# A fused transformer stack on one core: experts' first products between the quarters of a gather, and an embedding gate in unsplit full precision

## The chip, the core and the metric

The kernel runs on one core of a Trainium2 chip. Five engines work side by side, each through its own list of instructions in order: TensorE (PE; its weight loads are listed as PEld), VectorE (DVE), ScalarE (ACT), GpSimd (POOL) and SyncE (SP), which here only issues the transfers from memory (DMA). They wait for each other by semaphores. The metric is device time of one execution, in microseconds (us). Three runs of the kernel before took 1017.16, 1017.79 and 1019.13 us; the median is 1017.79.

## The reference

256 tokens (two blocks of 128) of width 1024, float32, go through five stages, each named by its result: a gated delta rule mixer with layernorm (x1), a mixture of experts with layernorm (x2), an embedding gate (x3), an "even" layer of mLSTM and pooling (x4) and an "odd" layer of sparse attention (the output). The change touches the second and third:

```
# mixture of experts: best of 4 groups, then the 2 best of its 8 experts
comb = g_onehot[:, :, None] * within[:, None, :]
for grp in range(MOE_GROUPS):
    h = silu(einsum("td,edf->tef", xt, w_gate[grp])) * einsum("td,edf->tef", xt, w_up[grp])
    out = out + einsum("tef,efd->td", h * comb[:, grp, :, None], w_down[grp])
x = _layernorm(DEEPNORM_ALPHA * x + h, ln_g[i, 1], ln_b[i, 1])                   # x2
x = x + jax.nn.sigmoid(x @ pe_w_gate[i]) * (p[i] @ pe_w_proj[i])                 # x3
```

## The kernel before

All stages are one program. Its order is not written out by hand: when the program is built, small generators (one for each piece of work) run under a planner that keeps a model clock for each engine and, where several pieces could go next, takes the one of the best number in the table `PRIO` (lower first; L40). What it decides becomes the fixed list of each engine.

**Weights** come in units of 128x1024 float32 (512 KB). `_load` (L518) walks through the list of all units in order: each waits for a free place (tiles named `raw`, `hl`, `first`, `moe_raw` (shown as la, xh_raw, xl_raw or moe_raw), `moe_hl`; the trace's names are those of the places), and SP issues its transfer. Because SP keeps the order of the list, a unit that waits for a place holds all behind it. Most weights are then split by `_split` (L542) into a high part in the rounded type fp32r (a cast, on ACT or DVE) and the low rest (a subtract, on DVE or POOL), and a product x@W is made of three fp32r products: high by high, low by high, high by low. A unit marked `full` isn't split and enters PE as float32, in full precision: the experts' units are of that kind.

**Mixture of experts.** The experts are worked on in eight sets of four, two for each group. `gather` (four quarters c per group) collects the tokens of the group's experts by products with a selection matrix `sel`, and copies each quarter into the tiles X. `back` transposes `sel` for the way back. `up(i)` runs over four steps j: each needs four units `m_gu` and quarter j of the gathered tokens, does eight products and gives the four places free. `down(i)` does the same with eight units `m_dn`, `scatter` brings the results back to the tokens and, after the last set, sums up for the layernorm that gives x2. `S.quiet` (L2285) tells `_split` to stay away from certain engines until an event.

**Embedding gate.** `Embed.main` takes eight units `p_gate`, `turn` transposes x2 in halves of 512 columns for each block of tokens and splits it into `xh` (ACT) and `xl` (DVE), and `block_slabs` does, per block of tokens (tb), 4 slabs x 8 steps of three fp32r products 128x256, 192 in all. `Embed.out` adds the gate to x2. The event `parted` lets no unit of the even layer be split before all `p_gate` units have their split's places. `e_v`, `e_za`, `e_qk` are the first units of the even layer.

In the trace, L207 are PE's products, L227 its transposes, L130 the operations of ACT, DVE and POOL, L178 ACT's table loads, and L232 the transfers.

Of the kernel before, what the change touches and what calls it, by code (L numbers as in the profile page):

```python
# [10 lines left out]
F32 = mybir.dt.float32  # L11
F32R = mybir.dt.float32r
I32 = mybir.dt.int32
AF = mybir.ActivationFunctionType
# [9 lines left out]
def size(ap):  # L24
# [14 lines left out]
}  # L39
PRIO = {  # L40
    "decay": [2, 3], "pick": 4, "base": 1, "lev": 1, "solve": 7, "qk": [2, 3], "v": 5, "z": 6,
    "m_turn": 2, "ranks": 1, "gather": 4, "back": 4, "slot_w": 6, "rest": 6, "act_out": 1, "scatter": 3,
    "m_const": 2, "parts": 1, "router": 3, "norm2": 1, "e_turn": 1, "embed": 7, "e_gates": 1, "gated": 2,
    "e_const": 2, "tokens": 3, "e_head": 3, "e_conv": 3, "window": 0, "e_out": 1, "keys": 1, "normed": 2,
    "copy": 2, "o_head": 2, "o_const": 2, "select": 2, "attend": 3, "o_gate": 1, "queries": 1, "o_out": 1,
# [6 lines left out]
QUIET = 0  # L52
QUIET_ON = [("dve", "pool"), ("dve",)]
SECOND = 15
SCRATCH = 1024
COST = {"parts": 2.5, "decay": 0.4, "conv": 2.8, "conv_qk": 3.0, "conv_v": 0.0, "gate": 0.65}

# [346 lines left out]
class Unit:  # L404
# [4 lines left out]
    def __init__(self, name, src, more="", n=1024, whole=False, late=False, full=False,  # L409
                 places=None):  # L410
        self.name, self.src, self.more, self.n, self.whole, self.late = name, src, more, n, whole, late
        self.full, self.low, self.places = full, False, places or ("raw", more + "raw", *(["first"] if more == "moe_" else []))
        self.sent, self.loaded, self.parted = Event(), Event(), Event()
        self.ready = self.loaded if whole or full else Event()
        self.raw = self.h = self.l = None

# [4 lines left out]
class Env:  # L421


    def __init__(self, tc, aps, ctx):
# [9 lines left out]
        S.slot_class("hl", self.wp, 6)  # L434
        S.slot_class("bank", self.psp, 4)
        S.slot_class("dbank", self.psp, 4)

    def gate_slots(self):

        s = self.S.slots  # L440
        s["gate_hl"] = s["moe_raw"] + s["moe_hl"]
        self.S.pools["gate_hl"] = self.S.pools["moe_raw"]
        held = [x for _, x in self.S.held.values() if x.cls in ("moe_raw", "moe_hl")]
        for x in s["gate_hl"] + held:
            x.cls = "gate_hl"
        self.S.drop("moe_raw", "moe_hl")

    def consts(self):
        nc, c, aps = self.nc, self.const, self.a
# [91 lines left out]

    def _split(self, u):  # L542
        S = self.S
        if u.more == "even_":

            yield Wait(*[v.parted for v in self.units[0:u.index] if v.more == "gate_"])
        hl = yield Alloc(("hl", u.more + "hl"), [1024], F32R, 2)
        S.set(u.parted)
        yield Wait(u.loaded)
        if u.full:  # L550
            S.free(*hl)
            return
        u.h, u.l = hl
        if u.more in ("moe_", "gate_"):

            late = Event()
            late.time = u.loaded.time + S.tune["slack"]
            yield Wait(late)
        near = u.index - self.at <= 1
        e = yield from self.outside(u, act=0.96, dve=0.61 + S.tune["high"][near])  # L560
        if u.full:
            S.free(*hl)
            return
        h, l, raw = u.h[:, 0:u.n], u.l[:, 0:u.n], u.raw[:, 0:u.n]
        if e == "act":
            S.s.activation(h, raw, AF.Copy)
        else:
            S.v.tensor_copy(h, raw)
        near = u.index - self.at <= 1
        e = yield from self.outside(u, dve=1.14 + S.tune["low"][near], pool=2.3)  # L570
        if u.full:
            S.free(*hl)
            return
        u.low = True
        S.of(e).tensor_tensor(l, raw, f32(h), op=OP.subtract)
        S.free(u.raw)
        S.set(u.ready)
# [1485 lines left out]
class Moe:  # L2063
# [215 lines left out]
    def scatter(self, i, y):  # L2279
        K, S = self.K, self.S  # L2280
        g, q = divmod(i, 2)
        last = i == 7
        if last:
            yield Wait(*self.done[0:7])
            S.quiet = QUIET_ON[1], ("p_gate",), self.bn_ev[1]  # L2285
            for n in range(2):
                S.spawn(self.start(0, n), "scatter")
        ys = yield Alloc("ys", [2, 512], F32R, 2)
        yield "act"
        for n in range(2):  # L2290
            S.s.activation(ys[0][:, n], y[n], AF.Copy)
        for n in range(2):
            yield "dve"
            S.v.tensor_tensor(ys[1][:, n], y[n], f32(ys[0][:, n]), op=OP.subtract)
            S.free(y[n])
        yield Wait(self.r_ev, self.selT_ev[g])
        selT = self.selT[g]
        for tb in range(2):
            for n in range(2):
                if last:  # L2300
                    yield Wait(self.sum_ev[tb][n])
                    p = self.sum[tb][n]
                else:
                    p = yield Alloc("bank", [512])
                yield "pe"
                for a in range(2):
                    S.mm(p, selT[:, q, tb, :], ys[a][:, n], a == 0 and not last, a == 1)
                if last:
                    S.set(self.sc_ev[tb][n])
                    if tb == 0:  # L2310
                        S.spawn(self.start(1, n), "scatter")
                    continue
                yield "dve"
                r = self.r[tb][:, 512 * n:512 * n + 512]
                S.v.tensor_tensor(r, r, p, op=OP.add)
                S.free(p)
        S.free(*ys)
        if q == 1:
            S.free(self.selT.pop(g))
# [130 lines left out]
def moe_units(a, K):  # L2450
    def unit(name, src):
        return Unit(name, src, "moe_", full=True, places=RAWS)

    def gu(i):
        return [unit("m_gu", lambda h=h, j=j: a["m_gu"][4 * i + h, :, 2 * j:2 * j + 2])
                for j in range(4) for h in range(4)]

    def dn(i):
        return [unit("m_dn", lambda h=h, k=k: a["m_dn"][4 * i + h, :, k]) for k in range(2) for h in range(4)]

    out = [Unit("m_r", lambda: a["m_r"], "moe_", 288, True)]
    for i in range(9):
        if i == 6:
            out += [Unit("pT", lambda: a["pT"], "moe_", 512, True)]
            out += [Unit("p_proj", lambda k=k: a["p_proj"][0, :, k], "moe_", whole=True) for k in range(2)]
        if i == 7:
            out += [Unit("lnr", lambda j=j: K.ln_row(1, j), "moe_", 1024, True) for j in range(2)]
        out += (gu(i) if i < 8 else []) + (dn(i - 1) if i > 0 else [])
    return out + [Unit("p_gate", lambda i=i, h=h: a["p_gate"][i, :, 4 * h:4 * h + 4], "gate_", places=("raw", "first")) for i in range(4) for h in range(2)]


class Embed:
# [6 lines left out]
        self.x_free = Event()  # L2479

    def turn(self, tb, c, x, ev):
        yield Wait(self.M.x2_ev[tb])
        yield from self.K.turn(self.M.x2[tb], tb, *x, 4 * c, ev)

    def main(self):
        K, S = self.K, self.S
        self.x2, self.pp = self.M.x2, self.M.E.pp
        x = K.parts()
        ev = [Event() for _ in range(4)]
        for tb in range(2):  # L2490
            for c in range(2):
                S.spawn(self.turn(tb, c, x, ev[2 * tb + c]), "e_turn")
        done = []
        yield from K.block_slabs(["p_gate"] * 4, x, ev,
                                 lambda i, tb, bank: done.append(S.spawn(self.out(i, tb, bank), "embed")))
        S.set(self.x_free)
        yield Wait(*done)
        S.free(self.x2, self.pp)

# [506 lines left out]
def build(tc, aps, upto="out", start="x1"):  # L3006
    nc = tc.nc
    run = ORDER[ORDER.index(start):ORDER.index(upto) + 1]
    with ExitStack() as ctx:
# [33 lines left out]
        if "x2" in run:  # L3043
            S.tune = TUNE["x2"]
            if "x1" not in run:
                K.moe_slots()
                E = Entry(K)
                E.lg = E.tile("lg", [2, 36])
                nc.sync.dma_start(E.lg, aps["lg"])
                for e in E.x1_ev + E.lg_ev:  # L3050
                    e.time = 0.0
                E.start(x)
            with ExitStack() as st:
                M = Moe(K, st, E)
                done = S.spawn(M.main(), 5)
                S.run(done)
                K.gate_slots()
                x, x_ev, free = M.x2, [[e, e] for e in M.x2_ev], ev[0]
                if "x3" in run:
                    E = Embed(K, M)  # L3060
                    x, x_ev, free = E.x3, E.x3_ev, E.x_free
                    if "x4" in run:
                        inp = K.rms_input(x, x_ev, "e_norm", free)
                    S.run(S.spawn(E.main(), 1))
                else:
                    S.run(M.x2_ev[0])
                    S.run(M.x2_ev[1])
                S.drop(*M.classes)
            S.drop("gate_hl", "first")
            K.moe_ctx.close()  # L3070
            K.first_ctx.close()
        S.tune = TUNE["x4"]
# [40 lines left out]
```

## Time and profile before

| | |
|---|---|
| median of three runs | 1017.79 us |
| profiled execution, its own time | 1019.82 us |
| its span (first to last instruction) | 1018.0 us |
| mean clock granted to PE | 0.973 |
| busy: PE, DVE, ACT, POOL | 956.3, 612.6, 485.1, 136.4 us |
| moved by DMA | 205.39 MB, mean 202 GB/s |

The profile is of one execution. Its busy times are sums over stages with different limits, so they don't tell what a stage waits for; the windows (busy time of each engine in a stretch, PE's granted clock, where 1.00 is 2.4 GHz and 0.50 is 1.2 GHz, DMA's share and rate) and the timelines do. In a timeline a row is one instruction or a run of like ones, with its start, its duration, and in square brackets the idle time ahead of it on its engine and what ended that. A full-precision product leaves two records in the trace. The stages lie about as follows: x1 to 360 us, the experts to 592, the embedding gate to 624, the even layer to some 900, the odd layer to the end.

### The profile page before, as it was taken

Reading aid. Unit: us, or ns where it says so; the run is one execution under the profiler, and the core shown is the slowest. Engines: PE = TensorE matmul, PEld = TensorE weight load, DVE = VectorE, ACT = ScalarE, POOL = GpSimd, SP = SyncE. Lnnn points to the kernel's source line nnn. Section 1 sums busy time; section 2 is a strip of 40 time slices with the busy share of each in tenths; the row PEclk is TensorE's granted clock in tenths of the full one; section 3 lists DMA queues with packets and bytes.
Section 4 is the critical chain, followed back from the end, with each engine's and each line's share of the span. In section 5 each row is a group of like instructions: output and inputs, shape, how many; then the busy total and the mean of one; then the engine's idle time right before and its main releaser. Section 6 shows DMA issues by size and latency. Waiting matters only on the chain. (4 is left out here: it accounts for less than half of the span.)

```text
span 1018.0 us, 17221 instructions
## 1 busy us (share of the span) xinstructions
PE 956.3 (94%) x6841; PEld 734.4 (72%) x6841; DVE 612.6 (60%) x1132; ACT 485.1 (48%) x904; POOL 136.4 (13%) x140
## 2 busy tenths in 40 slices
PE   8999879999799999999887889999999999998998
PEld 7778768888588754424221268999999988986886
DVE  7978964689956531221111287697677756587673
ACT  3888584893245222111100156566665444546561
POOL 2233232312000000000000081000000000005230
PEclk9999979999899989999998979999999999999999
DMA  6423411133738599999999853544444555633221
GB/s 224 146 83 105 163 33 56 63 104 125 277 106 327 212 369 397 409 409 409 408 410 407 334 194 117 179 164 156 160 146 166 166 185 164 255 111 104 84 95 51
DMA packets 56680, 205.39 MB, mean 202 GB/s; under 512 B 6416, under 2 KB 6800, under 8 KB 56208
## 3 DMA queue, kind: packets, MB, share of 16 engines
q1 hardware_dynamic: 56304, 204.02, 54.8%
q8 instruction: 56, 0.92, 0.4%
q14 instruction: 32, 0.26, 0.1%
q10 hardware_dynamic: 288, 0.19, 0.1%
HBM read 203.14 MB, written 1.05 MB: 201 GB/s over the span
## 5 line engine op out<-in xcount | busy, mean ns | idle before, releaser
L207 PE MATMUL dbank<-xh,hl 128*128 128x256 f32 x1072 | 217.0, 294 | 0.0
L207 PEld LDWEIGHTS dbank<-xh,hl 128*128 128x128 f32 x1072 | 172.7, 192 | 7.5 <-issue 5.8
L207 PE MATMUL dbank<-xl,hl 128*128 128x256 f32 x536 | 151.9, 283 | 0.0
L130 DVE TENSOR_TENSOR hl<-raw,hl 128x1024 fp32r<-128x1024 f32 x100 | 122.7, 1233 | 37.2 <-ACT hl L130 34.9
L130 ACT ACTIVATE hl<-raw 128x1024 fp32r<-128x1024 f32 x90 | 94.8, 1057 | 71.0 <-PE dbank L207 44.3
L207 PE MATMUL dbank<-hl,xh 128*128 128x256 f32 (+1 forms) x512 | 121.2, 321 | 1.0 <-ACT xh L130 1.0
L207 PEld LDWEIGHTS dbank<-xl,hl 128*128 128x128 f32 x536 | 103.0, 192 | 4.2 <-issue 4.1
L207 PEld LDWEIGHTS dbank<-hl,xh 128*128 128x128 f32 x512 | 89.2, 200 | 8.2 <-issue 1.9
L207 PE MATMUL dbank<-hl,xl 128*128 128x256 f32 (+1 forms) x256 | 80.9, 316 | 0.9 <-DVE xl L130 0.8
L178 ACT ACT_TABLE_LOAD x51 | 65.4, 1283 | 0.9
L207 PE MATMUL dbank<-first,raw 128*128 128x256 f32 (+1 forms) x260 | 61.7, 402 | 0.2 <-DMA first<-in_m_gu 0.2
L130 POOL TENSOR_TENSOR hl<-raw,hl 128x1024 fp32r<-128x1024 f32 x16 | 38.6, 2414 | 117.7 <-ACT hl L130 111.7
L207 PEld LDWEIGHTS dbank<-hl,xl 128*128 128x128 f32 x256 | 51.3, 200 | 3.7 <-DVE xl L130 1.4
L207 PEld LDWEIGHTS dbank<-first,raw 128*128 128x128 f32 (+1 forms) x260 | 47.0, 185 | 8.9 <-DMA first<-in_m_gu 1.8
L130 DVE TENSOR_TENSOR t<-t,t 128x31 f32<-128x31 f32 (+15 forms) x124 | 47.7, 385 | 4.3
L130 DVE SCALAR_TENSOR_TENSOR h<-h,cg,dbank 128x256 f32<-128x256 f32 x8 | 3.8, 480 | 77.1 <-ACT h L130 77.1
L130 DVE TENSOR_TENSOR moe_raw_m<-moe_raw_m,bank 128x512 f32<-128x512 f32 x28 | 18.9, 685 | 47.8 <-PE bank L207 47.8
L130 ACT ACTIVATE h<-dbank 128x256 f32<-128x256 f32 x16 | 5.9, 382 | 79.8 <-PE dbank L207 79.7
L130 DVE TENSOR_TENSOR ys<-dbank,ys 128x512 fp32r<-128x512 f32 x16 | 10.9, 689 | 46.4 <-ACT ys L130 46.2
L130 POOL TENSOR_TENSOR hl<-la,hl 128x1024 fp32r<-128x1024 f32 x3 | 7.1, 2371 | 228.0 <-DMA la<-in_p_gate 228.0
L130 ACT ACTIVATE ys<-dbank 128x512 fp32r<-128x512 f32 x16 | 9.4, 597 | 50.3 <-PE dbank L207 39.8
L207 PE MATMUL bank<-sel,x 128*128 128x256 f32 x128 | 32.1, 410 | 0.6 <-DVE sel L130 0.6
(512 smaller groups left out, 2136.0 us busy)
## 6 DMA issues: line engine op xcount, KB each, us to landing
la<-in_m_gu SPq DMA_DIRECT2D x40, 512.0 KB, 10.2
first<-in_m_gu SPq DMA_DIRECT2D x23, 512.0 KB, 10.2
hl<-in_m_gu SPq DMA_DIRECT2D x20, 512.0 KB, 10.2
moe_raw_m<-in_m_gu SPq DMA_DIRECT2D x20, 512.0 KB, 10.2
raw<-in_g_qk SPq DMA_DIRECT2D x16, 512.0 KB, 4.9
raw<-in_g_z SPq DMA_DIRECT2D x16, 512.0 KB, 3.5
raw<-in_g_v SPq DMA_DIRECT2D x16, 512.0 KB, 3.5
moe_raw_m<-in_m_dn SPq DMA_DIRECT2D x16, 512.0 KB, 10.1
```

The lines of the kernel that those rows point to most:

```text
L130: r = f(*a, **k)
L178: self.nc.scalar.preload_act_table_set(t)
L207: self.nc.tensor.matmul(out, lhsT, rhs, start=first, stop=last, skip_group_check=True)
```

## The change

Two things. In `PRIO`, `gather` goes from 4 to 6 and `back` from 4 to 7, so that the planner prefers an expert's products (priority 5, that of `Moe.main`) to the next quarter of the gather and to the transposes. And the units `p_gate` become `full`: they aren't split, `turn` transposes x2 and makes one float32 copy of each half (ACT or DVE) in place of `xh` and `xl`, and `main` does 64 products 128x256 in float32 itself. With this `parted` and `gate_slots` go (splits of the even layer no longer wait for those of the gate), and `S.quiet` after the last set of experts now keeps DVE and POOL from splitting `e_v` and `e_za` until the second block's statistics are done.

```diff
-    "m_turn": 2, "ranks": 1, "gather": 4, "back": 4, "slot_w": 6, ...
+    "m_turn": 2, "ranks": 1, "gather": 6, "back": 7, "slot_w": 6, ...
...
+PLACES = ("first", "moe_raw", "moe_hl")
...
     def _split(self, u):
         S = self.S
-        if u.more == "even_":
-
-            yield Wait(*[v.parted for v in self.units[0:u.index] if v.more == "gate_"])
         hl = yield Alloc(("hl", u.more + "hl"), [1024], F32R, 2)
-        S.set(u.parted)
...
-            S.quiet = QUIET_ON[1], ("p_gate",), self.bn_ev[1]
+            S.quiet = QUIET_ON[0], ("e_v", "e_za"), self.bn_ev[1]
...
-    return out + [Unit("p_gate", ..., "gate_", places=("raw", "first")) ...]
+    return out + [Unit("p_gate", ..., "gate_", full=True, places=PLACES) ...]
...
     def turn(self, tb, c, x, ev):
+        S, x2 = self.S, self.M.x2[tb]
         yield Wait(self.M.x2_ev[tb])
-        yield from self.K.turn(self.M.x2[tb], tb, *x, 4 * c, ev)
+        p = yield Alloc("bank", [4, 128])
+        yield "pe"
+        for i in range(4):
+            S.tr(p[:, i], x2[:, 512 * c + 128 * i:512 * c + 128 * i + 128], self.K.ident)
+        o = x[:, :, 128 * tb:128 * tb + 128]
+        e = yield Any(act=0.6, dve=0.69)
+        if e == "act":
+            S.s.activation(o, p, AF.Copy)
+        else:
+            S.v.tensor_copy(o, p)
+        S.free(p)
+        S.set(ev)
...
-        yield from K.block_slabs(["p_gate"] * 4, x, ev,
-                                 lambda i, tb, bank: done.append(S.spawn(self.out(i, tb, bank), "embed")))
-        S.set(self.x_free)
+        banks = yield Alloc("dbank", [2, 256], n=4)
+        us = [[K.unit("p_gate") for _ in range(2)] for _ in range(4)]
+        for tb in range(2):
+            for i, bank in enumerate(banks):
+                for half, u in enumerate(us[i]):
+                    yield Wait(u.ready, ev[2 * tb + half])
+                    w = u.raw.rearrange("p (k n) -> p k n", k=4)
+                    yield "pe"
+                    for k in range(4):
+                        S.mm(bank[:, tb], x[half][:, k, 128 * tb:128 * tb + 128], w[:, k], k == half == tb == 0,
+                             half == 1 and k == 3)
+                    if tb:
+                        S.free(u.raw)
+                done.append(S.spawn(self.out(i, tb, bank), "embed"))
```

The planner turns this into other lists of instructions. On PE, at the first group's gather, the list was as follows before (bank is a quarter of the gather, dbank the sum of the first set of experts, first and la are places of weight units, moe_raw_m the gathered tokens):

```order
L207 MATMUL bank_3701<-sel_3632,x_3280 128x256 x4
L207 MATMUL bank_3702<-sel_3632,x_3280 128x256 x4
L207 MATMUL bank_3703<-sel_3632,x_3280 128x256 x4
L207 MATMUL bank_3720<-sel_3632,x_3280 128x256 x4
L227 MATMUL bank_3726<-identr,sel_3632 128x128 x4
L207 MATMUL dbank_3635<-first_2728,moe_raw_m_3630 32x512 x2
L207 MATMUL dbank_3635<-la_3195,moe_raw_m_3630 32x512 x2
```

and is now:

```order
L208 MATMUL bank_3701<-sel_3632,x_3280 128x256 x4
L208 MATMUL bank_3702<-sel_3632,x_3280 128x256 x2
L208 MATMUL dbank_3635<-first_2728,moe_raw_m_3630 32x512 x2
L208 MATMUL dbank_3635<-la_3195,moe_raw_m_3630 32x512 x2
L208 MATMUL dbank_3635<-first_2728,moe_raw_m_3630 32x512 x2
L208 MATMUL dbank_3635<-la_3195,moe_raw_m_3630 32x512 x2
L208 MATMUL bank_3702<-sel_3632,x_3280 128x256 x2
L208 MATMUL bank_3703<-sel_3632,x_3280 128x256 x2
L208 MATMUL dbank_3635<-la_3195,moe_raw_m_3630 32x512
```

A quarter and a half are gathered, then the eight products of step j=0 follow, and the rest of the gather is mixed with the next steps; the transposes of `sel` come later.

On ACT, behind the sums of the last set of experts, the list was (st_6289 and st_6290 are the statistics of the first and the second block of tokens, la, first and moe_hl are units `p_gate` and their parts, xh<-bank the cast of the transposed x2):

```order
L130 ACTIVATE st_6289<-st_6289,eps_97 128x1
L130 ACTIVATE st_6289<-st_6289 128x1
L130 ACTIVATE moe_hl_6374<-first_2728 128x1024
L130 ACTIVATE first_2728<-dbank_6337,st_6289 128x320
L130 ACTIVATE moe_raw_m_6376<-first_2728 128x1024
L130 ACTIVATE moe_raw_m_6378<-la_3195 128x1024
L130 ACTIVATE moe_raw_m_6380<-la_3195 128x1024
L130 ACTIVATE xh<-bank_6393 128x4x128
L130 ACTIVATE xh<-bank_6394 128x4x128
```

and is now, with raw_6245 and raw_6255 the two units `e_v`, raw_6262 the first `e_za`, and moe_hl_6367<-bank_6377 the copy of the first half of the transposed x2:

```order
L131 ACTIVATE st_6289<-st_6289 128x1
L131 ACTIVATE first_2728<-dbank_6337,st_6289 128x320
L131 ACTIVATE hl_6259<-raw_6245 128x1024
L131 ACTIVATE hl_6293<-raw_6255 128x1024
L131 ACTIVATE st_6290<-st_6290,eps_97 128x1
L131 ACTIVATE st_6290<-st_6290 128x1
L131 ACTIVATE moe_hl_6367<-bank_6377 128x4x128
L131 ACTIVATE hl_6309<-raw_6262 128x1024
```

The casts of `p_gate` are gone, and the casts of both `e_v` stand ahead of the second block's statistics and of the copy.

On PE, at the start of the gate, two sets of four transposes and fp32r products in threes stood (hl_6259 and hl_6260 are a unit's high and low part):

```order
L227 MATMUL bank_6393<-identr,first_2728 128x128 x4
L227 MATMUL bank_6394<-identr,first_2728 128x128 x4
L207 MATMUL dbank_6389<-hl_6259,xh 128x256
L207 MATMUL dbank_6389<-hl_6259,xl 128x256
L207 MATMUL dbank_6389<-hl_6260,xh 128x256
L207 MATMUL dbank_6389<-hl_6259,xh 128x256
```

and now full-precision products in fours (la and first as moving operand are unsplit units, moe_hl_6367 and first_2728 as the other the halves of x2):

```order
L228 MATMUL bank_6377<-identr,first_2728 128x128 x4
L228 MATMUL bank_6378<-identr,first_2728 128x128 x4
L208 MATMUL dbank_6373<-la_3243,moe_hl_6367 128x256 x4
L208 MATMUL dbank_6373<-la_3243,first_2728 128x256 x4
L208 MATMUL dbank_6374<-la_3299,moe_hl_6367 128x256 x4
L208 MATMUL dbank_6374<-first_2728 128x256 x4
L208 MATMUL dbank_6375<-first_2728,moe_hl_6367 128x256 x4
L208 MATMUL dbank_6375<-la_3195,first_2728 128x256 x4
L208 MATMUL dbank_6376<-la_3195,moe_hl_6367 128x256 x4
L208 MATMUL dbank_6376<-la_3243,first_2728 128x256 x4
L228 MATMUL bank_6409<-identr,la_3320 128x128 x4
L228 MATMUL bank_6410<-identr,la_3320 128x128 x4
```

Each slab of the first block takes its two units one after the other, and the second block's transposes stand behind the first block's last product.

## Rows read from the trace of the kernel before

**Rows 1.** Page: the 40 slices (25.45 us each), data rate.

```profile
GB/s 224 146 83 105 163 33 56 63 104 125 277 106 327 212 369 397 409 409 409 408 410 407 334 194 117 179 164 156 160 146 166 166 185 164 255 111 104 84 95 51
```

**Rows 2.** Windows by stage; columns: busy us of each engine, clock, DMA share, GB/s.

```profile
386.00:576.00 190.00, 171.54 (x874) 56.30 (x872) 34.34 (x58) 25.55 (x57) 0.00 (x0) 0.98 1.03 409
595.20:601.70 6.50, 6.31 (x28) 6.02 (x29) 3.98 (x4) 4.10 (x7) 5.68 (x5) 0.50 0.43 173
601.70:623.80 22.10, 21.33 (x176) 20.91 (x176) 19.54 (x23) 9.45 (x19) 9.15 (x4) 1.00 0.23 74
631.90:900.00 268.10, 267.31 (x1960) 251.72 (x1959) 188.29 (x296) 147.41 (x237) 0.74 (x5) 1.00 0.52 174
900.00:1018.00 118.00, 108.33 (x671) 89.75 (x670) 77.65 (x163) 58.80 (x130) 33.50 (x39) 0.99 0.25 85
```

**Rows 3.** Chain of waits near the gate's end; columns: start us, us, what.

```profile
610.91 12.95 PE dbank L207 x106
```

**Rows 4.** SP timeline, the gather; columns: start us, us, engine, line, operation, tiles, count.

```profile
366.44 0.33 SPq L232 DMA_DIRECT2D xh_raw<-in_m_gu  x1
376.14 0.80 SPq L232 DMA_DIRECT2D first<-in_m_gu  x2
```

**Rows 5.** PE timeline, the gather of group 0 (records, two to a product).

```profile
363.64 10.20 PE L207 MATMUL bank<-sel,x 128*128 128x256 f32 x32 [0.55 <-DVE sel L130]
...
374.20 0.62 PE L207 MATMUL dbank<-first,moe_raw_m 128*32 128x512 f32 x2
...
382.07 7.17 PE L207 MATMUL bank<-sel,x 128*128 128x256 f32 x32
```

**Rows 6.** Windows at the gather of group 0.

```profile
370.00:374.00 4.00, 4.00 (x21) 3.51 (x20) 0.00 (x0) 1.32 (x3) 0.00 (x0) 1.00 1.02 411
374.00:386.00 12.00, 12.00 (x93) 5.77 (x92) 0.00 (x0) 3.62 (x6) 0.00 (x0) 1.00 0.83 292
```

**Rows 7.** ACT timeline, the copy of the gather's first quarter.

```profile
367.45 0.60 ACT L130 ACTIVATE moe_raw_m<-bank 128x512 f32<-128x512 f32 x1 [3.44 <-PE bank L207]
```

**Rows 8.** ACT timeline, the start of the gate.

```profile
588.46 1.06 ACT L130 ACTIVATE hl<-la 128x1024 fp32r<-128x1024 f32 x1 [0.61 <-DMA la<-in_p_gate]
589.42 0.28 ACT L130 ACTIVATE st<-st,eps 128x1 f32<-128x1 f32 x1
589.73 0.20 ACT L130 ACTIVATE st<-st 128x1 f32<-128x1 f32 x1
...
594.62 1.06 ACT L130 ACTIVATE xh<-bank 128x512 fp32r<-128x512 f32 x2
```

**Rows 9.** PE timeline, the gate: transposes, first product, second half's transposes, a wait.

```profile
592.06 1.33 PE L227 MATMUL bank<-identr,first 128*128 128x128 f32 x5 [2.49 <-DVE first L130]
...
595.25 0.58 PE L207 MATMUL dbank<-hl,xh 128*128 128x256 f32 x1 [0.62 <-ACT xh L130]
...
607.16 0.60 PE L227 MATMUL bank<-identr,la 128*128 128x128 f32 x4
...
608.38 0.51 PE L207 MATMUL dbank<-moe_raw_m,xh 128*128 128x256 f32 x2 [0.38 <-POOL moe_raw_m L130]
```

**Rows 10.** SP timeline, transfers for the stage behind the gate.

```profile
585.53 1.62 SPq L232 DMA_DIRECT2D raw<-in_e_v  x2
588.51 28.01 SPq L232 DMA_DIRECT2D raw<-in_e_za  x2
```

**Rows 11.** DMA issues from 578 to 600 us, with median time to landing.

```profile
raw<-in_e_v SPq DMA_DIRECT2D x2, 512.0 KB, 10.6
```

**Rows 12.** Windows where the queue of transfers ends.

```profile
596.00:597.00 1.00, 1.00 (x5) 1.00 (x6) 1.00 (x2) 1.00 (x2) 1.00 (x1) 0.50 1.00 401
597.00:598.00 1.00, 1.00 (x6) 1.00 (x6) 1.00 (x1) 0.05 (x1) 1.00 (x1) 0.50 0.86 344
```

**Rows 13.** DVE timeline, the statistics of the first half of x2.

```profile
587.83 0.21 DVE L130 BATCH_NORM_AGGREGATE st<-st 128x2 f32<-128x12 f32 x1
```

**Rows 14.** PE timeline, full-precision products 128x256 early in the kernel.

```profile
8.03 3.62 PE L207 MATMUL dbank<-first,raw 128*128 128x256 f32 x16
```

More of the change, by code (lines that the diff above doesn't have):

```diff
@@ L41 @@
     "decay": [2, 3], "pick": 4, "base": 1, "lev": 1, "solve": 7, "qk": [2, 3], "v": 5, "z": 6,
-    "m_turn": 2, "ranks": 1, "gather": 4, "back": 4, "slot_w": 6, "rest": 6, "act_out": 1, "scatter": 3,
+    "m_turn": 2, "ranks": 1, "gather": 6, "back": 7, "slot_w": 6, "rest": 6, "act_out": 1, "scatter": 3,
     "m_const": 2, "parts": 1, "router": 3, "norm2": 1, "e_turn": 1, "embed": 7, "e_gates": 1, "gated": 2,
@@ L412, in __init__ @@
         self.full, self.low, self.places = full, False, places or ("raw", more + "raw", *(["first"] if more == "moe_" else []))
-        self.sent, self.loaded, self.parted = Event(), Event(), Event()
+        self.sent, self.loaded = Event(), Event()
         self.ready = self.loaded if whole or full else Event()
@@ L436, in __init__ @@
         S.slot_class("dbank", self.psp, 4)
[L438 to L446, printed above, removed]
     def consts(self):
@@ L2468, in moe_units @@
         out += (gu(i) if i < 8 else []) + (dn(i - 1) if i > 0 else [])
-    return out + [Unit("p_gate", lambda i=i, h=h: a["p_gate"][i, :, 4 * h:4 * h + 4], "gate_", places=("raw", "first")) for i in range(4) for h in range(2)]
+    return out + [Unit("p_gate", lambda i=i, h=h: a["p_gate"][i, :, 4 * h:4 * h + 4], "gate_", full=True, places=PLACES) for i in range(4) for h in range(2)]
 class Embed:
@@ L2487, in main @@
         self.x2, self.pp = self.M.x2, self.M.E.pp
-        x = K.parts()
+        tiles = yield Alloc(PLACES, [1024], F32, 2)
+        x = [t.rearrange("p (k t) -> p k t", k=4) for t in tiles]
+        S.set(self.x_free)
         ev = [Event() for _ in range(4)]
@@ L2491, in main @@
             for c in range(2):
-                S.spawn(self.turn(tb, c, x, ev[2 * tb + c]), "e_turn")
+                S.spawn(self.turn(tb, c, x[c], ev[2 * tb + c]), "e_turn")
+        banks = yield Alloc("dbank", [2, 256], n=4)
+        us = [[K.unit("p_gate") for _ in range(2)] for _ in range(4)]
         done = []
-        yield from K.block_slabs(["p_gate"] * 4, x, ev,
-                                 lambda i, tb, bank: done.append(S.spawn(self.out(i, tb, bank), "embed")))
-        S.set(self.x_free)
+        for tb in range(2):
[10 more added lines that the diff above has]
+                done.append(S.spawn(self.out(i, tb, bank), "embed"))
+        S.free(tiles)
         yield Wait(*done)
@@ L3056, in build @@
                 S.run(done)
-                K.gate_slots()
                 x, x_ev, free = M.x2, [[e, e] for e in M.x2_ev], ev[0]
@@ L3068, in build @@
                 S.drop(*M.classes)
-            S.drop("gate_hl", "first")
+            S.drop(*PLACES)
             K.moe_ctx.close()
```

## The prediction

> **What bounds the kernel now.** I read the page's slices first, then busy time by stage, then the engines' timelines at the two places that the change touches. In the slices the data rate stands near 409 GB/s from the 17th slice to the 22nd, with 369 and 397 in the 15th and 16th, and later it never comes back to that [rows 1]. The windows say the same by stage: from 386 to 576 us the transfers run at 409 GB/s with a DMA share of 1.03, so that stage ends when its bytes have come, while from 631.9 to 900 PE is busy 267.31 of 268.1 us [rows 2]. Between the two lies the embedding's gate, 595.2 to 623.8, where DMA has little to do and PE sets the time, its first 6.5 us at a clock of 0.50, the lower of TensorE's two levels, 1.2 GHz [rows 2]. The chain of waits has PE's products up to 610.91 + 12.95 = 623.86 there [rows 3]. So two things count: bytes that could have moved before 386, and when the last product of the gate ends. Whatever moves that end moves everything behind it, PE being full to 900.
>
> **The gather.** SP issues a weight unit at 366.44 and the next only at 376.14 [rows 4], because all places are full and are given back only by the first products of experts. These stand on PE behind the whole gather of group 0, which begins at 363.64 and takes 10.2 us for its 16 products (32 records); the first expert's product runs at 374.20 [rows 5]. What is still queued keeps the rate at 411 GB/s until 374; from 374 to 386 it is 292 [rows 6]. Against 409 that is 12 x 117 = 1.40 MB not moved, 3.4 us at 409 GB/s. By the DMA share (0.83 where 1.03 is full) it would be 12 x 0.20 / 1.03 = 2.3 us.
>
> After the change PE does six gather products, then the eight of the first four units, then more gather. The copy of the first quarter ran at 367.45 for 0.60 us [rows 7]; the two further gather products, at up to 0.85 each, end near 368.8, so the eight run from about 368.8 to 371.2, and the first places come free near 371.2 instead of 376.1. Four places are 4 x 512 KB, 5.1 us of transfers at 409 GB/s, and the next four follow two gather pairs later, before 375. The queue never runs dry, so the hole should close whole. PE loses nothing: it is busy 12.00 of 12 us there [rows 6], with the same products in another order. Bounds: 0 (places don't come in time) and 3.4; a loss is excluded, since no place comes free later than before. I take **-3.4**, nearest to the byte count, because PE uses units far faster than they come (16 units in the 7.9 us from 374.20 to 382.07 [rows 5], 0.49 us each against 1.28 for a transfer). From 386 to 576 bytes alone hold the stage, so the whole shift reaches its end.
>
> **The gate: what goes.** Eight casts on ACT of about 1.06 us [rows 8], their eight subtracts, the split of x2, and PE's waits for POOL (0.38 us at 608.38 and one like it [rows 9]). In their place stand one copy per half of x2, and 64 full-precision products 128x256 for 192 fp32r ones. The freed casts cost the kernel nothing before except through the order on ACT, which comes next.
>
> **The gate: when it begins.** Before, ACT reaches the copy of the transposed x2 at 594.62, and PE begins at 595.25 [rows 8, 9]. In the changed order ACT has, ahead of this copy, two casts of e_v, whose transfers were issued at 585.53 and 1.3 us later [rows 10] and take 10.6 us to land [rows 11]: near 596.1 and 597.5, which is also where the rate falls, from 401 to 344 GB/s [rows 12]. SP's order up to there is unchanged, so against the stage's end they come no earlier. In the old trace's times: second cast 597.5 to 598.56; two small instructions for the second half of the tokens, of the kind that took 0.28 and 0.20 [rows 8], to 599.1; the copy, 0.60, to 599.7; PE's first product at **599.75** instead of 595.25, +4.5 us. Queued behind the waiting cast stands also the normalisation of the second half, and thereby that half of x2; it is wanted only after 616.
>
> The Trainium skill states, in "TensorE: Matmul & The Clock Gate", section on the architectural detail, that the queues of ACT and DVE are strictly first in, first out. The trace agrees as far as it goes: the small instruction at 589.42 stands right behind the cast of 588.46 [rows 8], though DVE had its statistics ready at 587.83 + 0.21 [rows 13]. By the rule the gate begins at 599.75; could ACT pass the waiting casts, at about 593.8, which is the first rival's time.
>
> **The gate: how long it takes.** Eight full-precision products of that shape (16 records) took 3.62 us at the full clock [rows 14], 0.43 each without the last one's tail; the fp32r ones 12.95 us for 106, 0.122 each [rows 3]. At the full clock that is 64 x 0.43 = 27.5 us against 192 x 0.12 = 23.0; at the low clock twice these. PE's clock was 0.50 for the gate's first 6.5 us [rows 2] after a stretch with little work on PE; after the change there is still less, so I take 6.4 us at 0.50: 7.4 products. The first half's other 24.6 take 10.6, to 616.75. The eight transposes of the second half, which stood inside the first half's products (607.16 [rows 9]), now stand behind them, and the copy behind these: 1.25 us without products. Then 32 x 0.43 = 13.8, to 631.8: **8.0 later** than 623.86. Bounds: +4.5 (later start only, as if the products were no dearer and the 1.25 hidden) to 4.5 + 4.5 + 1.25 + 3 = +13 (3 for a second such spell at half the pace, of 6.4 us).
>
> **The rest.** The tail behind the gate has the same instructions. Casts and transfers for the next stage come earlier (the second e_za waits until 616 now [rows 10]), but PE is full from 631.9 on: 0. Near the kernel's end the planner changes the order of some casts and products. PE is busy 108.33 of 118 us there [rows 2], so 9.7 us is all that an order could give, and as much is the most I would grant it to cost; the work is the same and only a few rows move, so I take 0, with 1.5 either way in the range.
>
> **Sum.** -3.4 + 8.0 = +4.6 on the profiled execution's 1019.82 us (span 1018.0 and 1.82 around it): 1024.4. That execution lies 2.03 above the median of the runs, 1017.79, so the forecast is **1022.4**.
>
> **Rivals.** The first is on the other side: ACT's wait for e_v doesn't decide, because e_v lands before ACT comes to its casts. PE then begins at about 593.8 (transposes from 592.06 [rows 9], some 1.1 us for a half, copy 0.6), has the low clock to 600.2, ends the first half at 610.8, the second at 625.9: +2.0, with -3.4 a net -1.4, 1016.4. Had PE the full clock throughout, 593.8 + 27.5 + 1.25 = 622.55, -1.3, net -4.7, 1013.1. It decides once PE's first product comes before 599.75 - 4.6 = 595.15. For it: the casts and subtracts that are gone leave ACT and DVE free; against it: e_v hangs on the queue of transfers, full until 597 [rows 12].
>
> The second: the hole isn't regained, because the places that come free at 371 are not those SP wants next, or the bytes are lost at a later gather, whose products now mix with the experts' too. Then +8.0 alone, 1025.8. For it: after 376 the rate took until 386 to recover; against it: PE's pace of 0.49 us per unit.
>
> The third: what is saved around the gate (POOL's and DVE's subtracts, earlier casts for the next stage, another order at the end) is worth 4 us that the rows of a busy PE don't show: 1018.4. For it speaks only the unused 9.7 us at the end.
>
> **How the numbers follow.** Forecast 0.52, with a range of its own from 1020 to 1025; first rival 0.20, second 0.16, third 0.12. A measurement of this kernel can tell about 0.2%, 2 us, from no change: faster is under 1015.8, slower over 1019.8. The forecast gives slower 0.49 and same 0.03; the second rival slower 0.16; the first faster and same 0.10 each; the third 0.05, 0.04 and 0.03. Sums: faster 0.15, same 0.17, slower 0.68. The range takes in the second rival and most of the first: 1015.0 to 1026.5.
>
> **What would show it.** Right: no gap of SP between 366 and 376, 400 GB/s or more in the windows from 364 to the stage's end, and that end 3.4 us earlier; ACT idle before a cast of e_v, with that transfer as releaser, and PE before its first gate product waiting for ACT's copy; 64 products at 0.43; the last one 4 to 5 us later than now. Wrong: a first gate product within 2 us of the transposes, a gate shorter than 29 us, or a stage end that hasn't moved.

## The result, and the profile after

The changed kernel took 1022.87 us (median of 6 runs, 1022.24 to 1024.14) against 1017.74 us of the kernel before in the same comparison: ratio 1.0051, 95% interval 1.0041 to 1.0061. It is 5.1 us slower; 4.6 had been forecast. The profiled execution has a span of 1021.2 us.

The slices first, the data rate of the changed kernel; the 15th and 16th answer to the dent in [rows 1]:

```profile
GB/s 224 145 83 105 165 30 56 64 103 124 282 118 329 224 407 408 410 409 409 408 409 408 325 169 22 193 165 160 169 147 166 166 178 157 255 121 66 122 94 52
```

They are at 407 and 408 GB/s now. The 25th (612.7 to 638.3 us), at 22, is new; it begins with the gate's second half. SP's timeline at the gather shows why the dent is gone (start, duration, transfer), beside PE's:

```profile
366.56 0.33 SPq L233 DMA_DIRECT2D xh_raw<-in_m_gu  x1
368.98 0.80 SPq L233 DMA_DIRECT2D first<-in_m_gu  x2
```

```profile
362.57 4.54 PE L208 MATMUL bank<-sel,x 128*128 128x256 f32 x12 [0.55 <-DVE sel L131]
367.04 0.62 PE L208 MATMUL dbank<-first,moe_raw_m 128*32 128x512 f32 x2
...
368.90 1.99 PE L208 MATMUL bank<-sel,x 128*128 128x256 f32 x8
```

SP's gap of 9.7 us [rows 4] has become 2.4. The eight first products stand at 367.04 to 368.9, behind six gather products, and the windows (busy time of the engines, then clock, DMA share, GB/s) show that nothing is lost from 374 to 386, where 292 GB/s stood [rows 6]:

```profile
364.00:370.00 6.00, 6.00 (x31) 3.63 (x30) 1.74 (x9) 0.60 (x1) 0.00 (x0) 0.82 1.02 417
370.00:374.00 4.00, 4.00 (x27) 2.05 (x26) 0.00 (x0) 0.75 (x2) 0.00 (x0) 1.00 1.03 411
374.00:386.00 12.00, 12.00 (x104) 4.97 (x106) 0.48 (x1) 4.33 (x10) 0.00 (x0) 1.00 1.03 408
```

At the gate, ACT's timeline answers to [rows 8]:

```profile
585.17 0.62 ACT L131 ACTIVATE first<-dbank,st 128x320 f32<-128x320 f32 x1 [0.65 <-DVE st L131]
592.24 1.06 ACT L131 ACTIVATE hl<-raw 128x1024 fp32r<-128x1024 f32 x1 [6.45 <-DMA raw<-in_e_v]
593.53 1.06 ACT L131 ACTIVATE hl<-raw 128x1024 fp32r<-128x1024 f32 x1 [0.23 <-DMA raw<-in_e_v]
594.49 0.28 ACT L131 ACTIVATE st<-st,eps 128x1 f32<-128x1 f32 x1
594.80 0.20 ACT L131 ACTIVATE st<-st 128x1 f32<-128x1 f32 x1
594.95 0.60 ACT L131 ACTIVATE moe_hl<-bank 128x512 f32<-128x512 f32 x1
```

ACT does nothing for 6.45 us until the first e_v has landed, and the copy that PE needs stands four instructions further on. PE's timeline answers to [rows 9]:

```profile
584.47 1.02 PE L208 MATMUL bank<-ys,selT 128*128 128x512 f32 x2
586.11 0.77 PE L228 MATMUL bank<-identr,first 128*128 128x128 f32 x5 [0.62 <-DVE first L131]
587.76 0.55 PE L228 MATMUL bank<-identr,first 128*128 128x128 f32 x3 [0.89 <-POOL first L131]
595.60 3.78 PE L208 MATMUL dbank<-la,moe_hl 128*128 128x256 f32 x8 [7.29 <-ACT moe_hl L131]
599.17 3.11 PE L208 MATMUL dbank<-la,first 128*128 128x256 f32 x8
602.11 1.89 PE L208 MATMUL dbank<-la,moe_hl 128*128 128x256 f32 x8
603.84 1.89 PE L208 MATMUL dbank<-first 128*128 128x256 f32 x8
...
612.47 1.04 PE L228 MATMUL bank<-identr,la 128*128 128x128 f32 x8
613.76 1.99 PE L208 MATMUL dbank<-la,moe_hl 128*128 128x256 f32 x8 [0.25 <-ACT moe_hl L131]
...
627.68 1.95 PE L208 MATMUL bank<-rms,x 128*128 128x128 f32 x16
```

The x2 of the first block is transposed by 588.3, and PE then stands for 7.29 us. Eight records (four products) take 3.57 us from start to start at the low clock (595.60 to 599.17) and 1.73 at the full one (602.11 to 603.84). The chain of waits of the changed kernel runs through just this:

```profile
582.68 10.82 DMA raw<-in_e_v
...
594.95 0.61 ACT moe_hl L131
595.55 0.04 issue
595.60 17.04 PE dbank L208 x64
```

Two rows of the kernel before serve for the comparison, its last sum and the first row behind its gate:

```profile
588.54 1.03 PE L207 MATMUL bank<-ys,selT 128*128 128x512 f32 x2
...
623.68 1.95 PE L207 MATMUL bank<-rms,x 128*128 128x128 f32 x16
```

The last sum of the experts ends on PE at 585.49 (589.57 before), the gate begins 10.11 us behind it (5.68 before) and PE goes on to the row `bank<-rms,x` 32.08 us later (28.43 before). The gate's length is meant so here, from its first product to that row.

### The profile page after: what moved, and what is told of

Its sections match the earlier page's. It is cut to its first block, busy times and chain, and to the rows that moved or that the text cites. A ratio compares the mean times of both kernels' runs of the same rounds, so it can differ in the third digit from the quotient of the medians.

```text
span 1021.2 us, 17074 instructions
## 1 busy us (share of the span) xinstructions
PE 954.5 (93%) x6777; PEld 730.1 (71%) x6777; DVE 602.0 (59%) x1128; ACT 479.7 (47%) x897; POOL 116.4 (11%) x131
## 5 line engine op out<-in xcount | busy, mean ns | idle before, releaser
L131 ACT ACTIVATE hl<-raw 128x1024 fp32r<-128x1024 f32 x94 | 99.1, 1056 | 80.1 <-PE dbank L208 45.8
L208 PE MATMUL dbank<-hl,xh 128*128 128x256 f32 (+1 forms) x464 | 107.6, 315 | 0.4 <-ACT xh L131 0.4
L208 PEld LDWEIGHTS dbank<-hl,xh 128*128 128x128 f32 x464 | 78.3, 193 | 6.7 <-issue 1.9
L208 PE MATMUL dbank<-hl,xl 128*128 128x256 f32 (+1 forms) x232 | 71.6, 309 | 0.8 <-DVE xl L131 0.8
L208 PEld LDWEIGHTS dbank<-hl,xl 128*128 128x128 f32 x232 | 44.7, 193 | 2.9 <-DVE xl L131 1.0
L208 PEld LDWEIGHTS bank<-sel,x 128*128 128x128 f32 x128 | 24.4, 199 | 12.3 <-issue 8.4
```

The source lines that it names most:

```text
L131: r = f(*a, **k)
L208: self.nc.tensor.matmul(out, lhsT, rhs, start=first, stop=last, skip_group_check=True)
```

## The experiments

The theory: closing the hole gives time, and the gate loses more, by ACT's queue (a later begin), the low clock that follows the pause, and dearer products. Rivals: the hole is worth nothing; or the products alone are the loss, and ACT's wait only takes the place of another. All ratios are to the kernel before, run beside each.

**The parts apart.** The kernel before with two numbers of the table changed:

```diff
-    ... "gather": 4, "back": 4, ...
+    ... "gather": 6, "back": 7, ...
```

> The kernel before with the two numbers of the table alone (gather 6, back 7); the gate as before, split. Theory (the two parts add up; closing the hole in the transfers is worth what the trace of the changed kernel shows at the sums of the last experts, 4.1 us): 1013.7 us, ratio to before 0.996, with 400 GB/s and more from 364 to 386 us. Rival (the hole is worth little, and the stage's end came earlier because the gate's units are no longer split): 1017 or more.

Measured: 1017.13 us, ratio 0.9986 (0.9974 to 0.9997): faster by 1.4 us, not 4.1. Of the 4.1 us at the sums, 1.1 stood already at the gather's first product (363.64 before, 362.57 after), up to which nothing was changed. And the changed kernel with the old numbers, the same diff backwards:

> The changed kernel with the old numbers for gather and back, so the unsplit gate alone. Theory: the gate ends 8.0 us later than before and nothing gives it back, 1025.8 us (1025 to 1027), ratio 1.008, with ACT waiting some 6 us for e_v ahead of the copy. Rival (the hole is worth little): 1022 to 1023, as the changed kernel.

Measured: 1024.52 us, ratio 1.0060 (1.0045 to 1.0075): slower by 6.1 us, below the expected 8.0. The parts add up (-1.4 + 6.1 = 4.7 against 5.1), so the two don't help or hinder each other, but both are smaller than expected. In the trace of the first the hole is closed; in that of the second, which has the old gather, it is not as deep as in the profile shown before. A second profile of the kernel before was taken for that:

> The kernel before, unchanged, for a second profile of it. Theory (the profiled execution shown with it lay 2 us above the median because its gather of group 0 ran longer at the low clock): the rate from 374 to 386 us is higher than 292 GB/s, the hole 1 to 2.5 us instead of 3.4. Rival: the hole is 3.4 us in every execution.

The windows from 364 to 386 of these three (gather alone, gate alone, the kernel before again), and last the one during the gather of the profile shown before:

```profile
364.00:370.00 6.00, 6.00 (x37) 3.34 (x39) 2.16 (x11) 1.19 (x2) 0.00 (x0) 1.00 1.02 408
374.00:386.00 12.00, 12.00 (x112) 4.70 (x100) 0.48 (x1) 3.90 (x9) 0.00 (x0) 1.00 1.03 408
```

```profile
364.00:370.00 6.00, 6.00 (x22) 5.01 (x21) 2.10 (x10) 1.19 (x2) 0.00 (x0) 0.72 1.02 418
374.00:386.00 12.00, 12.00 (x89) 6.64 (x82) 0.00 (x0) 2.49 (x5) 0.00 (x0) 1.00 0.90 329
```

```profile
364.00:370.00 6.00, 6.00 (x18) 4.87 (x18) 2.26 (x11) 0.94 (x2) 0.00 (x0) 0.61 1.02 414
374.00:386.00 12.00, 12.00 (x94) 6.13 (x87) 0.00 (x0) 3.28 (x5) 0.00 (x0) 1.00 0.84 316
```

```profile
364.00:370.00 6.00, 6.00 (x15) 4.66 (x15) 2.64 (x14) 0.61 (x2) 0.00 (x0) 0.52 1.02 405
```

With the old order the rate behind the gather was 292, 316 and 329 GB/s where the clock during it was 0.52, 0.61 and 0.72: a slower gather frees places later. By 409 GB/s these are holes of 3.4, 2.7 and 2.3 us; with the new order there is none at a clock of 1.00 here nor of 0.82 in the changed kernel. From the gather's first product to the last sum the old order took 225.9, 224.5 and 224.6 us, the new one 222.9 and 222.6. So the new order gains 3.0 to 3.3 us against the execution from which the 3.4 was read, and 1.6 to 2.0 against the two others. The expectation for the second profile was half met: the rate is higher, but the hole of 2.7 us is more than the 1 to 2.5 expected. And its theory falls: this execution took 1021.17 us, 3.4 above the median of 1017.76 beside it, with a shallower hole. What lifts an execution above the median is thus not mainly that hole.

**The order on ACT alone.** The changed kernel, with the casts of the even layer's units held in the planner until the first block's copies stand:

```diff
@@ Env._split
+        if u.more == "even_":
+            yield Wait(self.x2_turned)
         near = u.index - self.at <= 1
@@ Embed.turn, behind the copy
+        self.left -= tb == 0
+        if tb == 0 and self.left == 0:
+            S.set(self.K.x2_turned)
```

> The changed kernel with one wait more in the planner: the even layer's units are cast only after both halves of the first block's x2 have been copied, so on ACT the casts of e_v stand behind the copy instead of ahead of it; nothing else moves. Theory (ACT's queue, held by e_v's transfer, sets the gate's begin): PE's first gate product comes 7 us earlier against the sums than in the changed kernel (3.1 us behind the end of the sums instead of 10.1), 1016 us if PE's clock still falls to 0.50 at the gate's start, 1013 if it stays at 1.00. Rival (the dearer full-precision products are the loss, PE would have waited for the transfers of p_gate anyway): 1021 to 1023.

Measured: 1014.42 us, ratio 0.9958 (0.9942 to 0.9973). What was 5.1 us slower is 4.3 faster (0.0042 of 1018.38) by holding the casts of e_v behind the copy. The time lies between the two that the theory gave, 1013 and 1016. ACT and PE of this run, as above:

```profile
588.94 0.60 ACT L131 ACTIVATE moe_hl<-bank 128x512 f32<-128x512 f32 x1
590.25 0.62 ACT L131 ACTIVATE la<-bank,st 128x320 f32<-128x320 f32 x1 [0.71 <-DVE st L131]
592.99 1.06 ACT L131 ACTIVATE hl<-raw 128x1024 fp32r<-128x1024 f32 x1 [2.13 <-DMA raw<-in_e_v]
```

```profile
589.59 1.99 PE L208 MATMUL dbank<-la,moe_hl 128*128 128x256 f32 x8 [0.35 <-ACT moe_hl L131]
591.42 1.89 PE L208 MATMUL dbank<-la,first 128*128 128x256 f32 x8
```

ACT still waits for e_v, but nobody waits for ACT. (The second block's normalisation came ahead of the casts too, 590.25 instead of 596.39; PE wants that block only after 600.) The gate begins 3.18 us behind the sums instead of 10.11, and PE's clock stayed at 1.00 in this execution: 29.12 us long instead of 32.08. Together that is 9.9 us in the traces and 9.5 by the two ratios; the medians, taken at two times, differ by 8.5. The rival of the dearer products falls: they are all still there, and from the last sum to the gate's end this version takes 32.30 us where the split gate took 34.11.

**The second block's transposes** one slab earlier:

```diff
@@ Embed.main (tr_ev is set in turn, behind the transposes)
             for i, bank in enumerate(banks):
+                if tb == 0 and i == 3:
+                    yield Wait(*self.tr_ev[1])
```

> As the run with the casts behind the copy, and the second block's eight transposes put ahead of the last slab of the first block on PE. Theory: PE no longer waits for the copy between the two blocks, 0.5 us less than that run (the transposes' own 0.7 us stay on PE). Rival: the transposes hold PE up for the second block's x2, as much or more than is saved: the same or 0.5 us more.

Measured: 1014.30 us, ratio 0.9955 (0.9936 to 0.9975), no difference from the run before it. Its profiled gate was even 1.2 us longer, 30.29, and the window shows a lower clock at the gate's start, the first of the two rows being the run before, the second this one:

```profile
590.00:594.00 4.00, 4.00 (x20) 3.52 (x19) 1.07 (x3) 1.62 (x2) 1.77 (x3) 1.00 1.02 416
```

```profile
590.00:594.00 4.00, 3.98 (x11) 3.22 (x12) 1.50 (x3) 1.06 (x2) 1.77 (x3) 0.57 1.03 418
```

With the same pause on PE ahead of it (3.18 us behind the sums, with the same transposes in it) the clock fell in one execution and not in the other. The 0.5 us can't be told from that.

**The clock by itself.** Products without use (`bank<-farf,identr`, 128x512) were put into PE's pause, some behind the sums and some behind the first block's transposes (`up[0]`). The first attempts, with the numbers for the changed kernel:

```diff
+    def fill(self, n):
+        K, S = self.K, self.S
+        p = yield Alloc("bank", [512])
+        yield "pe"
+        for i in range(n):
+            S.mm(p, K.identr, K.far[0][:, None, :].to_broadcast([128, 4, 128]), True, True)
+        S.free(p)
...
+        yield from self.fill(2)
...
+        yield Wait(*self.up[0])
+        yield from self.fill(24)
```

> The changed kernel with its wait left as it is, but PE filled meanwhile: 2 products without use behind the sums, 24 between the first block's transposes and the gate. It separates the two things that the waiting costs. Theory: the gate begins as late as in the changed kernel (10 us behind the sums), but at the full clock, so its length falls from 32.1 to 29.1 us: 1019.9. Rival (all of what was won by putting the casts behind the copy was the begin itself): 1022 to 1023.

> The run with the casts behind the copy (two blocks' transposes as there), with idle PE time filled: 2 products without use 128x512 right behind the sums and 4 between the first block's transposes and the gate's first product. Theory (the clock of the gate's start is what differed between the two earlier runs with the casts behind the copy, 1.00 in one and 0.57 in 590 to 594 in the other): the clock stays at 1.00 there, the gate takes 29.1 us from first to last product, 1013 to 1014.5. Rival (the fill delays the transposes and the gate by its own 1.3 us and the clock wasn't the difference): 1015 to 1016.

> The kernel before with the new numbers for gather and back and its split gate, and with idle PE time filled: 8 products without use 128x512 behind the sums, 5 between the first block's transposes and the gate. Theory (the split gate loses some 3.2 us to the low clock, its first 6.5 us at 0.50): t of the gate's last product 3 us earlier against the sums, 1014 us, so as good as the unsplit gate with the casts behind the copy. Rival (the fill delays the transposes as much as the clock gives back): 1017.

Measured: on the changed kernel 1027.59 us, ratio 1.0092 (1.0073 to 1.0110), which neither theory had; with the casts behind 1014.79, 0.9968 (0.9956 to 0.9980), no gain; on the split gate 1015.63, 0.9977 (0.9965 to 0.9988), 1.5 us better than without a fill in the medians, though the intervals overlap and the traces show nothing of it: the gate began 8.76 us behind the sums instead of 5.65 and took 25.41 us instead of 28.53, the same sum. It could hardly be less, for what sets the end of the split gate there is POOL. In the kernel before the chain of waits reaches the products of [rows 3] from POOL's last three subtracts, and with the fill PE waits for POOL at the same place:

```profile
603.27 7.59 POOL moe_raw_m L130 x3
```

```profile
606.70 0.50 PE L207 MATMUL dbank<-moe_raw_m,xh 128*128 128x256 f32 x2 [0.82 <-POOL moe_raw_m L130]
```

PE gets POOL's last subtract 21.34 us behind the last sum in the kernel before, 21.40 with the new gather and 21.39 with the fill, and needs some 13 us from there to the end in each. A faster start of PE would only have lengthened its wait for POOL.

All three fills have one fault. PE of the first:

```profile
595.74 7.52 PE L208 MATMUL bank<-farf,identr 128*128 128x512 f32 x24 [7.17 <-ACT moe_hl L131]
603.10 1.24 PE L208 MATMUL dbank<-la,moe_hl 128*128 128x256 f32 x5
```

The fill had got the accumulator of a transpose, so it waited for the copy as well and then stood ahead of the gate for 7.4 us. Mended, the fill writes into an accumulator of the gate itself, which waits for nobody:

```diff
+        yield Wait(*self.up[0])
+        yield from self.fill(banks[0], 30)
```

> The changed kernel with its wait left as it is, and 30 products without use between the first block's transposes and the gate, into an accumulator of the gate, so that they run while ACT waits for e_v (in the earlier run of this kind they stood in the transposes' own place and waited for the copy too). Theory: the gate begins 10.1 us behind the sums as in the changed kernel, at the full clock, and takes 29.1 us instead of 32.1: 1019.9. Rival (what the casts behind the copy won was the begin alone): 1022 to 1023.

Measured: 1021.25 us, ratio 1.0035 (1.0022 to 1.0048), 1.6 us less than the changed kernel, 1.3 more than expected. PE and its clock:

```profile
588.70 7.07 PE L208 MATMUL dbank<-farf,identr 128*128 128x512 f32 x30
596.39 1.99 PE L208 MATMUL dbank<-la,moe_hl 128*128 128x256 f32 x8 [0.62 <-ACT moe_hl L131]
```

```profile
596.00:602.00 6.00, 5.61 (x26) 4.97 (x27) 5.97 (x6) 3.46 (x5) 3.74 (x3) 1.00 0.44 137
```

The begin is as late as in the changed kernel (10.28 us behind the sums) and the length is 29.12, so in the traces the low clock is 3.0 of the 9.9 us and the begin 6.9. That the medians give 1.6 and not 3.0 was not settled: the two intervals overlap, and stretches that no version touches vary by as much (the gather's first product stands at 362.0 to 364.4 us over all the profiles here). The same fill in the run with early transposes (5 products), and in the split gate with the new gather (7 and 5):

> The run with the casts behind the copy and the second block's transposes early, with 5 products without use between the first block's transposes and the gate, this time into an accumulator of the gate, which waits for no copy. Theory (a low clock at the gate's start is chance after the short pause, and costs some 1.2 us where it falls): clock 1.00 from the sums on, gate 28.7 us from first to last product, begin 3.2 us behind the sums, 1013.5. Rival (the fill delays as much as it saves): 1014.5 or more.

> The kernel before with the new numbers for gather and back and its split gate, with 7 products without use behind the sums and 5 between the first block's transposes and the gate, into an accumulator of the gate. Theory: the gate begins 5.7 us behind the sums as before, at the full clock, and takes 25.4 us, as in the earlier run with a fill, whose begin was 3 us late: 31.1 us from the sums to the last product instead of 34.2, 1013 to 1014. Rival: the second block's waits for POOL grow by what the clock gives, 1016 or more.

Measured: the first 1014.33 us, ratio 0.9969 (0.9959 to 0.9979): the clock was 1.00 throughout and the gate 28.50 us long, but it began 3.83 us behind the sums, and the time is that of the run without fill. It tells what the early transposes are worth in a trace: 28.50 us against 29.12 and 29.02 of the two gates with the casts behind the copy at the same clock, so about the 0.5 us expected of them, which the fill took back at the begin (0.65 us). The second took 1017.73 us, ratio 0.9998 (0.9989 to 1.0007), in the rival's range, though PE shows no wait for POOL there: the fill moved the planner's clocks, and ACT got the second block's statistics and a cast ahead of the two casts of the transposed x2, which ran at 591.34, 7.1 us behind the last sum of 584.28:

```profile
589.36 0.28 ACT L130 ACTIVATE st<-st,eps 128x1 f32<-128x1 f32 x1
589.67 0.20 ACT L130 ACTIVATE st<-st 128x1 f32<-128x1 f32 x1
589.78 1.04 ACT L130 ACTIVATE moe_raw_m<-la 128x1024 fp32r<-128x1024 f32 x1
590.83 0.62 ACT L130 ACTIVATE la<-bank,st 128x320 f32<-128x320 f32 x1
591.34 1.07 ACT L130 ACTIVATE xh<-bank 128x512 fp32r<-128x512 f32 x2
```

It is an order on ACT again, this time without a wait for a transfer: the gate began 7.70 us behind the sums instead of 5.65, its clock fell all the same (0.75 from 595 to 600), and it took 27.45 us. The trace shows 1.0 us lost from the last sum to the gate's end, and this execution took 1015.27 us; why the median lies 2.5 above that stays open. The fastest versions are those with the casts behind the copy, about 1014.4, faster than both kernels; none of their variants differs from another clear of the intervals.

## Why the prediction was right

*The gate's begin.* Named: ACT's order, held by e_v. Forecast in the old trace's times 599.75, less 3.4 for the earlier stage 596.35; the first product stood at 595.60, and against the last sum it came 4.4 us later than before, where 4.5 was forecast. The run with the casts behind the copy shows that this order is the cause: the copy's input was there at about 587 and its turn came at 594.95. That the casts stand on ACT at all comes with the change, whose `S.quiet` leaves the casts of e_v no other engine until the second block's statistics are done; no run with the unsplit gate had them on another. The Trainium skill states, in "TensorE: Matmul & The Clock Gate", section on the architectural detail, that ACT's queue is strictly first in, first out. The trace agrees: all four instructions between ran before the copy, in the list's order.

*The gate's length.* Forecast 631.8 - 599.75 = 32.05; measured 32.08. Each part fits: four products at 1.73 us from start to start, the low clock for 6.5 us at the beginning, 1.3 us for the second block's transposes and copy. One reading of the old gate was wrong, though no number rested on it: the prediction has PE set the time there, at a low clock for its first 6.5 us. The chain of waits ran through POOL up to 610.86, and a fill that spared PE the low clock moved the old gate's end by nothing. In the unsplit gate, which waits for no subtract, the low clock costs 3.0 us.

*The gate together.* From the last sum to the last product 34.1 us before and 42.2 after: +8.1, forecast +8.0. With the gate alone changed the trace has 41.7, +7.6, and the medians +6.1 (4.6 to 7.6); the second profile of the kernel before has 34.45, against which it is +7.2. Why the medians show less than the traces stays open. The first rival, that e_v would land in time, didn't come about.

*The gather.* The mechanism was right, the places came free at 369 instead of 376 (371.2 forecast), and the rate never fell, so the second rival didn't come about either. The size was right for the execution read (225.9 us from the gather to the last sum before, 222.9 after) and too large for the typical one: the medians give -1.4 (-2.6 to -0.3), and two other profiles of the old order -1.6 to -2.0. The weak step is that one execution's hole was taken for the typical one, though its depth goes with the clock during the gather. Where the 2.03 us lay by which that execution was above the median isn't shown; the second profile, with the shallower hole, lay 3.4 above. That -3.4 and +8.0 were both too large for the medians, by about 2 each, kept the total near, 4.6 against 5.1: that closeness is luck.

*The rest.* Between the gate's end and the even layer's last stretch nothing changed (270.2 us before, 270.0 after, to the first `bank<-ki,qi`). The last stage took 124.1 us before and 123.5 after, but over all the profiles here 123.3 to 125.4 with either order, so its reordering shows no effect, and up to 2 us come and go there from one execution to the next. Between the two profiled executions the stretches that the change touches give +5.1 us (-3.0 and +8.1), all together +3.2 (span 1018.0 to 1021.2): 1.1 of the difference lies ahead of the gather, where nothing was changed.

## What to carry to other kernels

An instruction that waited for a transfer held all that stood behind it on its engine here; when a wait is taken out of a planner, look first at what moves ahead of the instructions that the critical engine waits for. What the pause cost was the pause (6.9 us) and the clock behind it (3.0). The low clock cost only where PE set the end: in the split gate, where POOL did, sparing it gained nothing in the trace. And a term read from one profile is that execution's: a second profile of the same kernel shows how far the same stretch differs (225.9 and 224.5 us here).

## What the runs showed that was not expected

PE's clock after a pause of the same make was not the same in every execution: behind 3.18 us with eight transposes in it the window 590 to 594 had 1.00 in one run and 0.57 in another, whose order on PE differs only later. And a fill meant to keep PE busy is worth nothing where it shares an accumulator with what PE waits for: 24 products that were to run from 588 ran from 595.74.
